# Folding adaLN's partial sums over partition halves with adding DMAs, and turning them later

## The chip, the cores and the metric

The kernel runs on one core of one Trainium2 chip. The metric is the device time of one execution in microseconds. The kernel before took 902.61 us, the median of three runs (901.67 to 902.88).

## The reference, cut to what matters

One layer over 256 tokens of width 2048 (D = 2048, E = 4096), in float32:

```python
h = rmsnorm(x, norm_g)
mod = silu(c) @ ada_w + ada_b            # (2048,) @ (2048, 6144)
shift, scale, gate = split(mod, 3)
h = h * (1 + scale) + shift
b_gate, c_gate, v, g = split(h @ w_in, 4)     # w_in: 2048 x 16384
y = b_gate * causal_conv3(c_gate * v) * silu(g)
x = x + gate * (y @ w_out)                    # w_out: 4096 x 2048
return rmsnorm(x, final_g)
```

The part that matters here is `silu(c) @ ada_w` for shift and scale: a product of one vector with a 2048 x 4096 matrix, whose result has to stand as one number for each channel, with the channels on the partitions, before the tokens of those channels can be multiplied with `w_in`.

## The kernel before, in words

TensorE works on float32 values split in two: a high part (a cast on ScalarE, `split_hi`) and a low part (a subtraction on VectorE, `split_lo`). Each product of a 128x128 weight block with a 128x256 token block is done three times: high weights with high tokens, high weights with low tokens, low weights with high tokens. `product` (line 526) issues one such matmul.

The 2048 input channels are 16 blocks of 128, called k = 0 to 15. adaLN's shift and scale are made in eight groups of two such blocks (`ADA`, k0 = 0, 2, ..., 14). The first group has code of its own; the other seven go through `ada_piece`, `ada_sums` and `ada_done`. For one group, `ada_w` comes in as eight pieces `at` (two 128-row slices each, lines 497 and 498, two DMAs for each piece on the SP queue). VectorE multiplies each slice by its 128 values of silu(c), one per partition, and adds it to `gv`, which is 128 partitions x 2 (shift, scale) x 256 channels (16 instructions for each group, lines 510 and 512). What is left is a sum over the 128 partitions. `ada_done` (line 514) does it by turning: four transposes on TensorE (line 519, one for each of shift and scale and for each of two channel blocks) put `gv` into the PSUM tile `tp_g` with channels on partitions, and VectorE sums the 128 columns of each (`reduce_sum`, line 521). `modulate` then adds the biases (line 348) and makes the tokens: two activations on ScalarE for the high tokens (line 352), and two instructions for each block on VectorE for the low ones (lines 356 and 359).

The main products over the first 16 column tiles of each quarter of `w_in` run in 16 banks (4 chunks `ch` x 4 quarters `q`), each in several parts: `plan()` (line 51 on) decides by its own costs which bank is worked on with which range k0:k1, so that banks run on whatever tokens are ready. A part is one opening of a PSUM bank; a bank that was opened before is seeded from `acc` (line 566) or added to it (line 555). These are 3072 matmuls, in the order in which `part` issues them, numbered 0 to 3071 below. Weights come in blocks of up to four k (48 matmuls), and `raw`, high and low parts have three buffers each.

By the plan, the tokens of group 8 (k = 8, 9) are first used by matmul 1128, those of group 10 by 1440, of group 12 by 1728 and of group 14 by 2016.

The order of the instructions on the queues around this is written out as strings of letters (lines 635 to 646). For VectorE: `s` is one addition to `gv`, `l` a low split, `r` the reduction of line 521, `m` the biases, `t` one of the four low-token instructions. For ScalarE: `h` is a high cast, `k` a copy of a bank to `acc`, `e` a seed, `t` a high-token activation. For SP: `w` is a load of weights and `a` one of adaLN's. Where the strings end or a kind is not in them, Tile's scheduler decides by its own timeline. That also holds for the place of the transposes among the matmuls, and for the last group's `r`, `m` and tokens.

GpSimd does nothing in this stretch. Later it folds the sums of the gate, which are needed on all partitions: seven rounds for each of four column groups, each round two DMAs on its own queue (lines 687 and 688, together all 256 KB of a tile moved to other partitions) and one addition (line 689).

Of the kernel before, what the change touches and what calls it, by code (L numbers as in the profile page):

```python
# [11 lines left out]
ALU = mybir.AluOpType  # L12

P = 128
# [103 lines left out]
def short_conv_layer(ctx: ExitStack, tc: tile.TileContext, x, c, norm_g, ada_w, ada_b, w_in, conv_w, w_out, final_g, out):  # L118
    nc = tc.nc
# [43 lines left out]
    after = mybir.DependencyInfo(mybir.DependencyClass.NoSync, mybir.DependencyReason.DATA)  # L163
# [26 lines left out]
    @contextmanager  # L190
    def of_kind(letter):

        traced = nc.cur_bb.bb.instructions
        n = len(traced)
        yield
        for ins in list(traced[n:]):
            lined_up.setdefault((ins.engine, letter), []).append(ins)

    def interleave(engine, letters):


        left = {k: iter(v) for (e, k), v in lined_up.items() if e == engine}
        front = None
        for letter in letters:
            ins = next(left[letter])
            if front is not None:
                tc.add_manual_dep(ins, front.name, after, reason="in the order of the letters")
            front = ins
# [52 lines left out]
    ident = const.tile([P, P], F32, tag="ident", name="ident")  # L261
# [99 lines left out]
    def modulate(k0, nk, sums):  # L361

        with of_kind("m"):
            add_biases(k0, nk, sums)
        with of_kind("t"):
            for k in range(k0, k0 + nk):
                high_tokens(k)
                low_tokens(k)
# [55 lines left out]
    for k in range(KT):  # L424
        c_k = silu_c[:, k : k + 1]
        at, gv = first_ada[k], gv0
        if k in ON_PE:
# [7 lines left out]
            at, gv = at[:, :, P : NK0 * P], gv0[:, :, P : NK0 * P]  # L435
# [45 lines left out]
        nc.vector.tensor_tensor(out=dst[:, :, 1, :], in0=y, in1=dst[:, :, 0, :].bitcast(F32), op=ALU.subtract)  # L481


    acc = {}
    sums = {}

    def ada_piece(k0, nk, piece):
        w = nk * P
        kk = ASLOT // (2 * w)
        if piece == 0:  # L490
            sums[k0] = adap.tile([P, 2, 2 * P], F32, tag="gv", name="gv")
        gv = sums[k0][:, :, 0:w]
        j = piece * kk
        at = adap.tile([P, ASLOT], F32, tag="at", name="at", bufs=4)
        at4 = at.rearrange("p (k s f) -> p k s f", k=kk, s=2)
        with of_kind("a"):
            for s in range(2):
                nc.sync.dma_start(at4[:, :, s, :], adas[:, j : j + kk, s, k0 * P : k0 * P + w])
        with later(GIVE), of_kind("s"):
            ada_sums(j, kk, at4, gv)  # L500
        if j + kk == KT:
            with later(-LEAD):
                ada_done(k0, nk, gv)
# [10 lines left out]
    def ada_done(k0, nk, gv):  # L514

        tp = psum.tile([P, 4, P], F32, tag="sm", name="tp_g", bufs=2)
        gs = const.tile([P, 4], F32, tag="gs", name="gs", bufs=2)
        for o in range(2 * nk):
            nc.tensor.transpose(tp[:, o, :], gv[:, o // nk, (o % nk) * P : (o % nk + 1) * P], ident)  # L519
        with of_kind("r"):  # L520
            nc.vector.reduce_sum(gs[:, 0 : 2 * nk], tp[:, 0 : 2 * nk, :], axis=mybir.AxisListType.X)
        modulate(k0, nk, gs[:, 0 : 2 * nk])

    opener = [None]

    def product(dst, hi, lo, k, i, begins, left, ends):

        w, h = ((hi, hh_), (hi, hl_), (lo, hh_))[i]

        mm = last_mm[0] = nc.tensor.matmul(dst, w, h[k], start=begins and left, stop=ends, skip_group_check=True)  # L530
        if begins and left:
            opener[0] = mm
        elif begins:
            tc.add_manual_dep(mm.ins, opener[0].ins.name, after, reason="the bank's flags are cleared first")

    def chunk_products(bank, hi, lo, o0, k, k0, k1, seed=False, late=False, parts=(0, 1, 2)):


        begins = k == k0 and not seed
        terms = [(m, i) for i in (0, 2, 1) for m in range(CT)] if late else [(m, i) for m in range(CT) for i in parts]  # L540
        for m, i in terms:
            o = slice(o0 + m * P, o0 + (m + 1) * P)
            product(bank[:, m, :], hi[:, o], lo[:, o], k, i, begins and i == 0, m % 2 == 0, 2 in parts and k == k1 - 1 and (m, i) == terms[-1])
# [72 lines left out]
    for kind, *step in plan():  # L616
# [15 lines left out]
                mixed(ch)  # L632


    interleave(mybir.EngineType.SP, (
        "wwaawaawaawaawwwaaaawwaaaawwaawaawaaaawaawwaawwaaaaaawwaawaaaaaawaawaawaaaawaawaawaaaawaawaawaawaaaa"
        "aawwaaaawaaaawwaaaawaawaaaawwaaaawaawaaaawaawaawaaaawaawaawaa"
    ))
    interleave(nc.vector.engine, (
        "lslsslslsslssllsslssllsssslslsrmslsttttslscsssslllssllssssssvlrmssltttstslssssslsslsslssssrlsmlsttst"  # L640
        "tslslsssssslslssslsrsmststttlslsssslslsssslslsrsmsslsttstltssslssslsslsssslsrmslsttttslsssslsslssls"
    ))
    interleave(nc.scalar.engine, (
        "hhhkxxxxhkhkkhkhhkhkhhkkhkhkhttkkhkhehhkhhkekehehkttekhekehkehkehkehkehttkhehkehhkhetthkhekehhkehhke"
        "htthkehhkehhkehtthkehhkhehkhehtthkehhkehhkehhkeh"
    ))

    ys.extend(slot([P, 2, 2, T], f"y{j}", F32R) for j in range(len(ys), NCT // 2))
# [72 lines left out]
    for ct in range(NS, NCT, 2):  # L721
        for q in QUARTERS:
            bank = psum.tile([P, CT, T], F32, tag="mm", name="mm_b")[:, 0:2]
            col = q * E + ct * P
            for kp in range(0, KT, KP):
                raw = raw_tile("raw")
                nc.sync.dma_start(
                    raw.rearrange("p (k f) -> p k f", k=KP),
                    w_in[0, kp * P : (kp + KP) * P, col : col + 2 * P].rearrange("(k p) f -> p k f", p=P),
                )  # L730
                hi, lo = split(raw, SLOT)
                for m in range(2):
                    for i in range(KP):
                        k = kp + i
                        o = slice((i * 2 + m) * P, (i * 2 + m + 1) * P)
                        for j in range(3):
                            product(bank[:, m, :], hi[:, o], lo[:, o], k, j, k == 0 and j == 0, m == 0, k == KT - 1 and j == 2)
                gate_piece()
# [137 lines left out]
    def wide_bank(name):  # L876
        return psum.tile([P, 2, W], F32, tag="mm", name=name)
# [32 lines left out]
    halves = [wide_bank("mm_o") for _ in range(2)]  # L910
# [89 lines left out]
```

## Time and profile before

| what | us |
|---|---|
| median of three runs | 902.61 |
| the profiled execution's own time | 902.57 |
| its span | 900.8 |
| TensorE busy | 887.4 (99%) |
| VectorE busy | 677.7 (75%) |
| ScalarE busy | 484.2 (54%) |
| GpSimd busy | 83.5 (9%) |

The page's names: PE is TensorE's matmuls, PEld its weight loads, DVE is VectorE, ACT ScalarE, POOL GpSimd, SP the queue that issues most DMAs. "Tenths" are rows of 40 digits, one for each fortieth of the span (22.5 us). A row of the timeline begins with the start and the duration, both in us, then engine, line, operation, output, input, and how many instructions were merged; square brackets at its end hold the idle time before it and what ended that. A row of the chain of work that ended last begins with start and duration too. Times in the text are counted from the start of the span.

### The profile page before, as it was taken

The numbers are of one execution on the slowest core, as the hardware profiler recorded it, in microseconds if no ns is written. First come the engines' busy times: TensorE is split into PE (matmuls) and PEld (weight loads), VectorE is DVE, ScalarE is ACT, GpSimd is POOL, SyncE is SP. The second block draws the span as 40 slices with busy tenths as digits, with TensorE's granted clock in tenths as the row PEclk, the third lists the DMA queues.
The fourth block names the chain that finished last, engine by engine and source line by source line (L and its number), as shares of the span: only waits on it lengthen the run. The fifth ranks groups of instructions, "written<-read, shape, count | busy, mean of one in ns | idle before, by whom it ended". The sixth has DMA issues, their size and how long they took to land.

```text
span 900.8 us, 16415 instructions
## 1 busy us (share of the span) xinstructions
PE 887.4 (99%) x6997; PEld 851.0 (94%) x6997; DVE 677.7 (75%) x667; ACT 484.2 (54%) x430; POOL 83.5 (9%) x95
## 2 busy tenths in 40 slices
PE   7999999999999999999999999999999999999996
PEld 4999999999999999999999999999999988888885
DVE  5899989888888867765965677555555568879896
ACT  6767966665558766644433434444434445554543
POOL 0000000000000134024234203320000000000000
PEclk9999999999999999999999999999999999999999
DMA  9999999999998588688888788766656476674662
GB/s 306 369 369 368 367 331 351 350 369 347 351 330 285 165 277 247 187 260 239 285 245 244 244 283 260 237 216 199 200 188 188 141 287 222 194 277 125 202 234 94
DMA packets 159610, 235.01 MB, mean 261 GB/s; under 512 B 6900, under 2 KB 105284, under 8 KB 159152
## 3 DMA queue, kind: packets, MB, share of 16 engines
q1 hardware_dynamic: 156368, 226.52, 76.6%
q0 software_dynamic: 3040, 7.39, 2.9%
q8 instruction: 55, 0.90, 0.4%
q14 instruction: 19, 0.16, 0.0%
q10 hardware_dynamic: 128, 0.04, 0.0%
HBM read 224.49 MB, written 2.10 MB: 252 GB/s over the span
## 4 chain that ended last, share of the span: by engine, by line
PE 95%; DMA 3%; DVE 1%; ACT 1%; issue 0%; SPq 0%; ACTq 0%
PE mm_s L530 39%; PE mm_b L530 39%; PE mm_w L793 7%; PE mm_o L793 6%; PE mm L793 4%; DMA at<-in_ada_w_dram 2%; DMA raw_o<-in_sc_w_out_dram 1%; PE tp_g L519 0%; PE sum L418 0%; ACT hi L380 0%; SPq L240 0%; DVE lo L824 0%; ACT hi L821 0%; DVE sums_o L816 0%; ACT big L907 0%
## 5 line engine op out<-in xcount | busy, mean ns | idle before, releaser
L530 PE MATMUL mm_b<-hT,hi 128*128 128x256 f32 x2048 | 348.2, 276 | 0.0
L530 PE MATMUL mm_s<-hT,hi 128*128 128x256 f32 x2048 | 336.6, 277 | 0.0
L530 PEld LDWEIGHTS mm_b<-hT,hi 128*128 128x128 f32 x2048 | 308.2, 188 | 0.0
L530 PEld LDWEIGHTS mm_s<-hT,hi 128*128 128x128 f32 x2048 | 299.1, 188 | 0.2
L530 PE MATMUL mm_b<-hT,lo 128*128 128x256 f32 x1024 | 282.6, 276 | 0.0
L530 PE MATMUL mm_s<-hT,lo 128*128 128x256 f32 x1024 | 261.8, 277 | 0.0
L385 DVE TENSOR_TENSOR lo<-raw,hi 128x2048 fp32r<-128x2048 f32 (+1 forms) x66 | 153.3, 2324 | 101.3 <-ACT hi L380 100.8
L380 ACT CAST hi<-raw 128x2048 fp32r<-128x2048 f32 (+1 forms) x66 | 123.7, 1875 | 192.7 <-PE mm_b L530 144.0
L530 PEld LDWEIGHTS mm_b<-hT,lo 128*128 128x128 f32 x1024 | 192.2, 188 | 0.0
L530 PEld LDWEIGHTS mm_s<-hT,lo 128*128 128x128 f32 x1024 | 182.5, 188 | 0.0
L385 DVE TENSOR_TENSOR lo<-raw_s,hi 128x2048 fp32r<-128x2048 f32 (+1 forms) x80 | 150.4, 1887 | 35.5 <-ACT hi L380 34.9
L380 ACT CAST hi<-raw_s 128x2048 fp32r<-128x2048 f32 (+2 forms) x81 | 124.0, 1540 | 59.4 <-PE mm_s L530 51.4
L512 DVE SCALAR_TENSOR_TENSOR gv<-at,silu_c,gv 128x512 f32<-128x512 f32 x105 | 78.6, 749 | 4.8 <-DMA at<-in_ada_w_dram 3.1
L552 ACT COPY acc<-mm_s 128x1024 f32<-128x1024 f32 x54 | 54.7, 1014 | 38.8 <-PE mm_s L530 38.7
L385 DVE TENSOR_TENSOR lo<-raw_o,hi 128x2048 fp32r<-128x2048 f32 x22 | 50.4, 2291 | 22.8 <-ACT hi L380 22.8
L380 ACT CAST hi<-raw_o 128x2048 fp32r<-128x2048 f32 x22 | 42.0, 1908 | 45.9 <-DMA raw_o<-in_sc_w_out_dram 10.1
L793 PE MATMUL mm_w<-hi,y 128*128 128x512 f32 x184 | 58.8, 389 | 0.0
L793 PE MATMUL mm_o<-hi,y 128*128 128x512 f32 x176 | 55.4, 389 | 0.0
L689 POOL TENSOR_TENSOR gacc<-gacc,z 128x512 f32<-128x512 f32 x28 | 42.3, 1511 | 105.5 <-DMA z<-gacc 105.5
L683 DVE SCALAR_TENSOR_TENSOR gacc<-at_g,silu_c,gacc 128x512 f32<-128x512 f32 x60 | 46.9, 781 | 6.5 <-DMA at_g<-in_ada_w_dram 5.3
L687 POOL DMA_DIRECT2D z<-gacc x28 | 15.5, 555 | 364.9 <-DVE acc L610 300.6
L793 PEld LDWEIGHTS mm_w<-hi,y 128*128 128x128 f32 x184 | 34.5, 188 | 7.1
(156 smaller groups left out, 687.9 us busy)
## 6 DMA issues: line engine op xcount, KB each, us to landing
raw<-in_sc_w_in_dram SPq DMA_DIRECT2D x64, 1024.0 KB, 5.8
raw_s<-in_sc_w_in_dram SPq DMA_DIRECT2D x47, 1024.0 KB, 7.8
raw_o<-in_sc_w_out_dram SPq DMA_DIRECT2D x32, 1024.0 KB, 5.3
at<-in_ada_w_dram SPq DMA_DIRECT2D x126, 256.0 KB, 7.7
raw_s<-in_sc_w_in_dram SPq DMA_DIRECT2D x33, 512.0 KB, 6.9
at_g<-in_ada_w_dram SPq DMA_DIRECT2D x32, 512.0 KB, 7.8
x<-in_x_dram SPq DMA_DIRECT2D x4, 512.0 KB, 6.4
big<-in_x_dram SPq DMA_DIRECT2D x2, 1024.0 KB, 8.2
```

The lines of the kernel that those rows point to most:

```text
L380: nc.scalar.copy(hi[:, :n], raw[:, :n])
L385: last_low[0] = nc.vector.tensor_tensor(out=lo[:, :n], in0=raw[:, :n], in1=hi[:, :n].bitcast(F32), op=ALU.subtract)
L512: nc.vector.scalar_tensor_tensor(out=gv, in0=at4[:, i], scalar=c_k, in1=gv, op0=ALU.mult, op1=ALU.add)
L530: mm = last_mm[0] = nc.tensor.matmul(dst, w, h[k], start=begins and left, stop=ends, skip_group_check=True)
L552: nc.scalar.copy(acc[ch, q], bank)
L683: nc.vector.scalar_tensor_tensor(out=ga, in0=at3[:, i, :], scalar=s, in1=ga, op0=ALU.mult, op1=ALU.add)
L687: nc.gpsimd.dma_start(turned[0 : P - away], ga[away:P])
L689: nc.gpsimd.tensor_tensor(out=ga, in0=ga, in1=turned, op=ALU.add)
L793: nc.tensor.matmul(dst, y[a], b, start=opens and i == 0, stop=ends and i == 2, skip_group_check=True)
```

## The change

For the last four groups (k0 = 8, 10, 12, 14; `FOLD = 8`) the 128 partial sums are first folded to 64. One DMA on GpSimd's queue adds the upper 64 partitions of the shift's sums to the lower 64. A second one adds the lower 64 partitions of the scale's sums to the upper 64. Each moves 64 rows of 1 KB. GpSimd then copies the folded scale (64 partitions x 256) beside the folded shift, into the partitions that became free. One transpose now turns shift and scale of one channel block together: two transposes for a group, where there were four. The reduction reads 256 columns of PSUM where it read 512.

The transposes of these groups get a fixed place: after the matmuls numbered 1034, 1284, 1534 and 1834, and ahead of the next one. In the written orders of VectorE and ScalarE the letters `r`, `m` and `t` of groups 8, 10 and 12 move back, behind some `s`, `l`, `h`, `k` and `e`; the order on SP stays.

```diff
+    FOLD = 8
+    TURNS = (1034, 1284, 1534, 1834)
+    turns = []
...
-        for o in range(2 * nk):
-            nc.tensor.transpose(tp[:, o, :], gv[:, o // nk, (o % nk) * P : (o % nk + 1) * P], ident)
+        if k0 >= FOLD:
+            h = P // 2
+            nc.gpsimd.dma_start(gv[0:h, 0], gv[h:P, 0], accum_op=ALU.add)
+            nc.gpsimd.dma_start(gv[h:P, 1], gv[0:h, 1], accum_op=ALU.add)
+            nc.gpsimd.tensor_copy(gv[h:P, 0], gv[h:P, 1])
+            turns.append([nc.tensor.transpose(tp[:, k, :], gv[:, 0, k * P : (k + 1) * P], ident) for k in range(nk)])
+            halves = tp[:, 0:nk, :].rearrange("p k (s f) -> p s k f", s=2)
+        else:
+            for o in range(2 * nk):
+                nc.tensor.transpose(tp[:, o, :], gv[:, o // nk, (o % nk) * P : (o % nk + 1) * P], ident)
+            halves = tp[:, 0 : 2 * nk, :].rearrange("p (s k) f -> p s k f", s=2)
         with of_kind("r"):
-            nc.vector.reduce_sum(gs[:, 0 : 2 * nk], tp[:, 0 : 2 * nk, :], axis=mybir.AxisListType.X)
+            nc.vector.reduce_sum(
+                gs[:, 0 : 2 * nk].rearrange("p (s k) -> p s k", s=2), halves, axis=mybir.AxisListType.X
+            )
...
+        products.append(mm)
...
+    for turned_rows, n in zip(turns, TURNS):
+        tc.add_manual_dep(turned_rows[0].ins, products[n].ins.name, after, reason="the folded sums are there")
+        tc.add_manual_dep(products[n + 1].ins, turned_rows[-1].ins.name, after, reason="no later")
...
     interleave(nc.vector.engine, (
         "lslsslslsslssllsslssllsssslslsrmslsttttslscsssslllssllssssssvlrmssltttstslssssslsslsslssssrlsmlsttst"
-        "tslslsssssslslssslsrsmststttlslsssslslsssslslsrsmsslsttstltssslssslsslsssslsrmslsttttslsssslsslssls"
+        "tslslsssssslslssslsssslrslmtststtsslslsssslslsssslssrlmssslttstsstlsslsssslsslsslrmssssttlttsslssls"
     ))
     interleave(nc.scalar.engine, (
-        "hhhkxxxxhkhkkhkhhkhkhhkkhkhkhttkkhkhehhkhhkekehehkttekhekehkehkehkehkehttkhehkehhkhetthkhekehhkehhke"
-        "htthkehhkehhkehtthkehhkhehkhehtthkehhkehhkehhkeh"
+        "hhhkxxxxhkhkkhkhhkhkhhkkhkhkhttkkhkhehhkhhkekehehkttekhekehkehkehkehkehttkhehkehhkhehkhettkehhkehhke"
+        "hhkehtthkehhkehhkttehhkhehkhehhketthhkehhkehhkeh"
     ))
```

More of the change, by code (lines that the diff above doesn't have):

```diff
@@ L517, in ada_done @@
         gs = const.tile([P, 4], F32, tag="gs", name="gs", bufs=2)
-        for o in range(2 * nk):
-            nc.tensor.transpose(tp[:, o, :], gv[:, o // nk, (o % nk) * P : (o % nk + 1) * P], ident)
+        if k0 >= FOLD:
[9 more added lines that the diff above has]
+            halves = tp[:, 0 : 2 * nk, :].rearrange("p (s k) f -> p s k f", s=2)
         with of_kind("r"):
-            nc.vector.reduce_sum(gs[:, 0 : 2 * nk], tp[:, 0 : 2 * nk, :], axis=mybir.AxisListType.X)
+            nc.vector.reduce_sum(
+                gs[:, 0 : 2 * nk].rearrange("p (s k) -> p s k", s=2), halves, axis=mybir.AxisListType.X
+            )
         modulate(k0, nk, gs[:, 0 : 2 * nk])
     opener = [None]
+    products = []
     def product(dst, hi, lo, k, i, begins, left, ends):
```

## The prediction, made before the result was known

> **What bounds the kernel now.** I read the page first: busy time, then the span in 40 slices.
>
> ```profile
> span 900.8 us, 16415 instructions
> PE 887.4 (99%) x6997; PEld 851.0 (94%) x6997; DVE 677.7 (75%) x667; ACT 484.2 (54%) x430; POOL 83.5 (9%) x95
> POOL 0000000000000134024234203320000000000000
> DMA  9999999999998588688888788766656476674662
> ```
>
> TensorE is busy 887.4 of 900.8 us, so almost every instruction taken off it shortens the span, and every wait put in front of it lengthens it. GpSimd shows no work in slices 2 to 13 (22 to 293 us), which hold the groups touched here. The DMA engines are full in just those slices. Next the chain of work that ended last, in order of time, for the place of each transpose; "x" counts matmuls, and no other engine appears in this stretch.
>
> ```profile
> 24.70 31.63 PE mm_s L530 x274
> ...
> 56.76 12.02 PE mm_s L530 x102
> 68.87 17.46 PE mm_s L530 x152
> ...
> 86.77 27.37 PE mm_s L530 x241
> ...
> 114.57 25.32 PE mm_s L530 x223
> 139.90 0.44 PE tp_g L519 x4
> 140.33 26.35 PE mm_s L530 x232
> ...
> 167.36 29.73 PE mm_s L530 x262
> ...
> 197.89 32.13 PE mm_s L530 x283
> ...
> 230.82 146.81 PE mm_s L530 x1295
> 377.63 348.16 PE mm_b L530 x3072
> ```
>
> Adding the counts numbers the matmuls: 274 + 102 + 152 + 241 + 223 = 992 stand ahead of group 8's transposes at 139.90 us; 232 more, 1224, ahead of group 10's; after a few mixed with single matmuls, 1491 are done at 197.89 and 1777 at 230.82. One matmul is 348.16 / 3072 = 0.1133 us, four transposes are 0.44 us (0.11 each). The new places are after numbers 1034, 1284, 1534 and 1834, some 43 to 60 matmuls (5 to 7 us) later.
>
> **The change, part by part.**
>
> (1) Fewer transposes. Eight go, 8 x 0.11 = 0.88 us off TensorE. There is no stall here to remove: from 24.70 to 377.63 TensorE is the chain throughout. Less work on VectorE follows:
>
> ```profile
> L519 PE MATMUL tp_g<-ident,gv x28: 270/272/273, 56.2 to 230.6; 128*128 128x128 f32 x28
> L521 DVE TENSOR_REDUCE gs<-tp_g x7: 683/691/692, 56.8 to 232.6; 128x4 f32<-128x512 f32 x7
> ```
>
> Half the columns make the reduction about 0.35 instead of 0.69 us, four times; VectorE isn't the bound, so nothing for the sum. (The 272 ns of one transpose is pipelined; the chain's 0.11 is what it adds.)
>
> (2) The fold, which is new on the path to the transposes. First its deadline, for group 8, from VectorE's timeline and ScalarE's:
>
> ```profile
> 136.14 0.74 DVE L512 SCALAR_TENSOR_TENSOR gv<-at,silu_c,gv 128x512 f32<-128x512 f32 x1
> 136.99 0.49 DVE L510 TENSOR_SCALAR gv<-at,silu_c 128x512 f32<-128x512 f32 x1
> ...
> 146.41 2.29 DVE L385 TENSOR_TENSOR lo<-raw_s,hi 128x2048 fp32r<-128x2048 f32 x1
> ```
> ```profile
> 143.48 1.09 ACT L352 ACTIVATE hT<-xs,mod 128x256 fp32r<-128x256 f32 x2 [3.44 <-DVE mod L348]
> 144.48 1.90 ACT L380 CAST hi<-raw_s 128x2048 fp32r<-128x2048 f32 x1
> ```
>
> The row at 136.99 opens group 10's sums, so group 8's last addition is the one at 136.14 and ends at 136.88. TensorE comes to its transposes after 43 matmuls more than before: 139.90 + 43 x 0.1133 = 144.8 (144.7 by the matmuls' own starts). So the fold has 7.8 us. Its pieces by their nearest rows, GpSimd's later folds of the gate:
>
> ```profile
> L689 POOL TENSOR_TENSOR gacc<-gacc,z x28: 1286/1295/3657, 313.7 to 591.3; 128x512 f32<-128x512 f32 x28
>   DMA z<-gacc: 105.5, 28
> ```
> ```profile
> L687 POOL DMA_DIRECT2D z<-gacc x28: 530/554/576, 310.7 to 586.5; - x28
> ```
> ```profile
> L688 POOL DMA_DIRECT2D z<-gacc x28: 502/510/524, 311.2 to 587.0; - x28
> DMA to landing us min/median/max: 2.3/4.1/8.7
> ```
> ```profile
> rows<-in_sc_conv_w_dram POOLq DMA_DIRECT2D x1, 48.0 KB, 5.5
> ```
> ```profile
> 137.00:141.00 4.00, 4.00 (x37) 4.00 (x36) 3.07 (x3) 3.04 (x3) 0.00 (x0) 1.00 1.06 376
> 141.00:145.00 4.00, 4.00 (x38) 4.00 (x37) 4.00 (x8) 1.52 (x3) 0.00 (x0) 1.00 1.08 364
> 545.00:562.00 17.00, 17.00 (x153) 17.00 (x152) 13.31 (x13) 6.79 (x5) 5.08 (x5) 1.00 0.92 276
> ```
>
> The first DMA is issued in 0.55 us; with some 0.2 us for the semaphore (an estimate; GpSimd's own turn-arounds are 0.3) the second starts at 137.65. From there 2.3, 4.1 or 8.7 us to landing: 139.9, 141.8 or 146.4. The DMA share (last column but one) says where in that range: 1.06 to 1.08 here, more than the 0.92 around the slowest gate folds (545 to 562 us). The one DMA that GpSimd issued in the crowded opening took 5.5 us for 48 KB. I take 5 us, 142.65. A gate pair moves 256 KB, this pair 128 KB, but an adding DMA also reads what it adds to, and no trace row shows one: it could be nothing dearer, or, if it serves its data twice, double. Then the copy: the addition of 512 columns and two inputs has 1.29 at least, the copy of 256 columns and one input should be half, 0.65 (0.3 to 1.3). It ends near 143.4, 1.3 us ahead of the deadline. I count this step at nothing; its cover is 42 matmuls, and beyond that each microsecond of delay is one of TensorE.
>
> A rule set against this. The Trainium skill, "DMA: Bandwidth & Descriptors", section "Anatomy of one DMA — SWDGE (gpsimd) path", prices such a DMA at 2.0 us plus bytes over 436e3, which for 64 KB is an estimate of 2.15 us. By it the fold would be in place near 140.5 and the sum would stay -0.88; by the slowest row above it would become a loss of about 1.4. The rows disagree with the rule, as their median is twice that.
>
> The other groups have more time. The last additions of groups 10, 12 and 14:
>
> ```profile
> 159.92 1.54 DVE L512 SCALAR_TENSOR_TENSOR gv<-at,silu_c,gv 128x512 f32<-128x512 f32 x2
> ...
> 189.67 0.74 DVE L512 SCALAR_TENSOR_TENSOR gv<-at,silu_c,gv 128x512 f32<-128x512 f32 x1
> ...
> 221.74 0.75 DVE L512 SCALAR_TENSOR_TENSOR gv<-at,silu_c,gv 128x512 f32<-128x512 f32 x1
> ```
>
> They end at 161.46, 190.41 and 222.49. The transposes come at 167.36 + 59 x 0.1133 = 174.0, 197.89 + 44 x 0.1133 = 202.9 and 230.82 + 58 x 0.1133 = 237.4, each less what the earlier groups have saved (up to 1 us): 11.5 to 14 us, against a fold of 0.75 + 8.7 + 0.65 = 10.1 at the slowest row. In group 12 the moved letters make VectorE up to 1.5 us later, which leaves 10. Nothing. On SP nothing is moved; the adding DMAs put some 0.5 MB into a stretch that moves 0.35 MB in each microsecond, 1.5 us over 100, behind loads that mostly wait for a free buffer. Nothing.
>
> (3) The later tokens. Group 8's are first used by matmul 1128, (1128 - 1035) x 0.1133 = 10.5 us after its new transposes. Behind these come the reduction, the biases, two activations and four vector instructions, queued behind at most one low split and one cast: about 5 us. The others have 17 us or more. Nothing.
>
> (4) The new order on VectorE. In group 8 it helps: the split at 146.41 stood behind the reduction and the tokens (and its cast at 144.48 behind ScalarE's wait of 3.44); now both pass them. The cast still needs the buffer that matmul 1007 frees, 140.33 + 16 x 0.1133 + 0.3 = 142.4, so the split can start at about 142.4 + 1.9 = 144.3, some 2 us earlier. That buffer is wanted by matmul 1080 at 140.33 + 88 x 0.1133 = 150.3, so VectorE was 1.6 us ahead and will be 3.6. In group 10 it hurts: the four token instructions (0.41 each) move to between two splits:
>
> ```profile
> 179.30 2.29 DVE L385 TENSOR_TENSOR lo<-raw_s,hi 128x2048 fp32r<-128x2048 f32 x1 [0.21 <-ACT hi L380]
> ...
> 183.75 2.28 DVE L385 TENSOR_TENSOR lo<-raw_s,hi 128x2048 fp32r<-128x2048 f32 x1
> ```
>
> The second ends at 186.03, is wanted by matmul 1416 at 167.36 + 190 x 0.1133 = 188.9, and becomes 1.65 us later: about 0.8 us stay. Nothing, but with little over.
>
> The sum: -0.88 + 0. Against the profiled execution's 902.57 (span 900.8 and 1.8 around it) that is 901.7; the profile lies 0.04 under the median of the three runs, so it holds for the median too.
>
> **The rivals.**
>
> (B) Group 8's fold is a little late. For: full DMA engines, an unknown price of adding. Against: 1.3 us of room. In its place a second mechanism makes the delay coarse: VectorE's next low split follows at about 144.3, by (4). In the gate's folds, GpSimd's addition took longest where such a split ran beside it:
>
> ```profile
> 548.35 3.66 POOL L689 TENSOR_TENSOR gacc<-gacc,z 128x512 f32<-128x512 f32 x1 [3.32 <-DMA z<-gacc]
> ```
> ```profile
> 548.56 2.28 DVE L385 TENSOR_TENSOR lo<-raw,hi 128x2048 fp32r<-128x2048 f32 x1
> ```
>
> It ended at 552.01, 1.17 after that split's end at 550.84, as if it had begun only then. So a copy that misses 144.3 ends near 144.3 + 2.3 + 0.5 = 147.1, a stall of 2.4: 901.7 + 2.4 = 904.1. The Trainium skill says the same in "SBUF — State Buffer", section "SBUF: two separate sides": VectorE with two SBUF inputs and a reading GpSimd instruction lock each other out for a whole instruction. By that rule this rival costs 2.4; without it, about 1 us less.
>
> (C) Slower: adding DMAs cost twice the plain ones. Place: TensorE ahead of group 8's transposes. With 2 x 5 us to landing the fold is there at 137.65 + 10 + 0.65 = 148.3 at the earliest, a stall of 3.6 and up to 2 more for a split in the way; groups 10 to 14 (0.75 + 10 + 0.65 = 11.4) just pass. 901.7 + 3.6 to 5.6 = 905.3 to 907.3. It decides from a landing of 9.2 us on, where the stall of 2.7 eats the gain and reaches 904.4. For: slices of full DMA. Against: only the data part, not the whole latency, should double.
>
> (D) Group 10's low split comes late, by letters. It decides from a delay of 0.8 us; price up to 1 us: 902.7.
>
> **How the numbers follow.** Forecast 0.50, B 0.25 (one in five of it over 904.4), C 0.15, D 0.06, and 0.04 for a gain that I see no place for. About 0.2% (1.8 us) is what a measurement of this kernel can tell from no change: under 900.8 is faster, over 904.4 slower. Forecast, D and most of B lie within, 0.76; C and the rest of B give 0.20; 0.04 faster. The range: below, the gain with the scatter of the three runs (0.6), 901.0; above, B's end, 904.6, which leaves C out.
>
> **What would show it.** Right: `tp_g` with 20 transposes instead of 28; four rows of GpSimd's copy, group 8's ending ahead of about 144.7; in the chain, TensorE unbroken from 24.70 to about 376.8; reductions of 0.35. B or C: TensorE with an idle time before `tp_g`, ended by GpSimd's copy, near 144.7, and landings of the adding DMAs over 6 us. D: an idle time near 188.5, ended by a low split. What would make it wrong outright is an adding DMA that is slower than any plain one here, in all four groups.

## The result, and the profile after

The changed kernel takes 907.18 us, the median of seven runs (906.1 to 912.0), against 902.36 before (901.67 to 902.98). The ratio is 1.0062, with a 95% interval of 1.0043 to 1.0081 (a ratio here compares single executions and isn't the quotient of the medians, which is 1.0053): 0.6% slower, where 901.7 was forecast, with a range of 901.0 to 904.6. The profiled execution took 906.1 us, 3.5 more than the profiled one before. It is the fastest of the seven, so 1.3 of the 4.8 us between the medians are not in its trace; the five slowest have a lower mean granted clock (0.994 to 0.996, where the two fastest have 0.997), which points to longer stretches at a low clock, but no trace of them was kept.

Two lines of the page of the changed kernel:

```profile
span 904.3 us, 16427 instructions
PE 888.7 (98%) x6989; PEld 851.7 (94%) x6989; DVE 674.4 (75%) x667; ACT 483.5 (53%) x430; POOL 101.3 (11%) x107
```

TensorE has eight instructions fewer, as it should, and is yet busy 1.3 us longer, beside 2.2 us more in which it isn't. The chain of work that ended last (start, duration, what) leaves TensorE around group 8, where it never did in the kernel before:

```profile
142.39 1.92 ACT hi L380
144.33 2.30 DVE lo L385
146.68 4.04 PE mm_s L545 x19
150.94 5.15 PE mm_s L545 x45
156.12 1.03 ACT acc L568
...
158.12 1.92 ACT hi L380
160.06 2.31 DVE lo L385
162.41 15.17 PE mm_s L545 x131
177.79 31.80 PE mm_s L545 x279
209.81 31.31 PE mm_s L545 x276
241.34 139.65 PE mm_s L545 x1232
380.99 348.36 PE mm_b L545 x3072
```

From 146.68 on, 19 matmuls take 4.04 us, 0.21 each where 0.113 is the rule. TensorE's timeline and its waits (us in total, times, longest) show what stands in front of them:

```profile
143.86 0.28 PE L545 MATMUL mm_s<-hT,lo 128*128 128x256 f32 x1
144.35 0.50 PE L545 MATMUL mm_s<-hT,hi 128*128 128x256 f32 x2 [0.22 <-ACT hi L380]
146.68 0.39 PE L545 MATMUL mm_s<-hT,lo 128*128 128x256 f32 x1 [1.82 <-DVE lo L385]
...
150.37 0.35 PE L545 MATMUL mm_s<-hT,lo 128*128 128x256 f32 x1
150.56 0.38 PE L526 MATMUL tp_g<-ident,gv 128*128 128x128 f32 x2
```
```profile
PE mm_s L545 <- DVE lo L385: 2.1, 2, 1.8
```

The wait isn't ahead of the transposes (`tp_g`, line 526 now), as the rivals B and C had it, but ahead of main products, and for a high cast and a low split. The order of TensorE's instructions in the two programs explains it. Matmul 1034 (the row at 143.86) is the last ahead of the transposes by the diff. In the built program Tile's scheduler put this there (each number in `mm_s_` is one bank; lines are in TensorE's order):

```
mm_s_1792<-hi_1795  x2
mm_s_1792<-lo_1796          matmul 1034
mm_s_1860<-hi_1863  x2      matmuls 1080, 1081: the next bank
mm_s_1860<-lo_1864
...                         18 more of the next bank, 1083 to 1100
tp_g<-gv            x2      group 8's transposes
mm_s_1792<-hi_1795          matmul 1035
```

So 21 matmuls of the next bank come between. (It also pulled 29 matmuls ahead of group 12's transposes and 5 ahead of group 14's; TensorE waits at neither in the trace.) In the kernel before they were 45 matmuls away, and VectorE had their weights 1.6 us ahead of them; here they are wanted at once:

```profile
142.39 1.91 ACT L380 CAST hi<-raw_s 128x2048 fp32r<-128x2048 f32 x1 [2.97 <-DMA raw_s<-in_sc_w_in_dram]
```
```profile
144.33 2.29 DVE L385 TENSOR_TENSOR lo<-raw_s,hi 128x2048 fp32r<-128x2048 f32 x1 [0.48 <-ACT hi L380]
```

The split ends at 146.62, and TensorE goes on at 146.68. The windows (length, busy time of PE, PEld, DVE, ACT and POOL, then the granted clock of TensorE, the DMA share, GB/s) give both halves of the loss:

```profile
143.80:146.70 2.90, 0.86 (x6) 0.46 (x5) 2.34 (x2) 2.90 (x4) 2.16 (x1) 1.00 1.07 372
146.70:150.50 3.80, 3.80 (x19) 3.80 (x20) 0.00 (x0) 0.37 (x1) 0.18 (x1) 0.55 1.08 364
161.80:163.00 1.20, 0.88 (x8) 0.68 (x7) 1.20 (x3) 1.07 (x2) 0.00 (x0) 1.00 0.07 19
```

TensorE stands still for 2.90 - 0.86 = 2.0 us. With the slow restarts, 2.6 us go there: from 143.86 to 146.91 four matmuls start, which take 4 x 0.1133 = 0.45 in a stream, 3.05 - 0.45. Then the granted clock is 0.55 in the mean of 3.8 us: 19 matmuls where 3.8 / 0.1133 = 33.5 fit, 14.5 x 0.1133 = 1.65 us. (It is 0.50 for 3.41 of them, see the last section.) Another 0.6 us go near 162, restart included. By the chain a low split is late there, because its cast stood behind the copy (`acc`, 156.12) of a bank that TensorE, itself late, had only then finished. That makes 4.9, less 0.9 for the eight transposes: 4.0. The measured difference of the two profiled executions is 3.5; 0.6 us of this gap lie ahead of group 8, as the chain goes on behind group 6's transposes at 113.94 here and at 114.57 in the kernel before.

The fold itself, GpSimd's timeline for group 8 and the copy for group 10, and the landings of all four second DMAs:

```profile
136.86 0.90 POOL L523 DMA_DIRECT2D gv<-gv  x1 [127.02 <-DVE gv L515]
137.45 1.17 POOL L524 DMA_DIRECT2D gv<-gv  x1
144.54 2.34 POOL L525 COPY gv<-gv 64x256 f32<-64x256 f32 x1 [5.93 <-DMA gv<-gv]
...
174.87 0.40 POOL L525 COPY gv<-gv 64x256 f32<-64x256 f32 x1 [5.50 <-DMA gv<-gv]
```
```profile
DMA to landing us min/median/max: 6.1/6.7/7.2
```

Group 8's sums are folded at 146.88, 2.9 us behind the 144.0 at which TensorE had done matmul 1034. So there are two candidates for the loss, one hidden behind the other: the order (theory O: the 21 matmuls that were pulled ahead and their weights) and the fold (theory F: it would have held TensorE up at the same place for as long).

### The profile page after: what moved, and what is told of

Its sections match the earlier page's. It is cut to its first block, busy times and chain, and to the rows that moved or that the text cites. A ratio compares the mean times of both kernels' runs of the same rounds, so it can differ in the third digit from the quotient of the medians.

```text
span 904.3 us, 16427 instructions
## 1 busy us (share of the span) xinstructions
PE 888.7 (98%) x6989; PEld 851.7 (94%) x6989; DVE 674.4 (75%) x667; ACT 483.5 (53%) x430; POOL 101.3 (11%) x107
## 4 chain that ended last, share of the span: by engine, by line
PE 92%; DMA 4%; DVE 2%; ACT 1%; issue 1%; SPq 0%; ACTq 0%
PE mm_b L545 39%; PE mm_s L545 36%; PE mm_w L812 7%; PE mm_o L812 6%; PE mm L812 4%; DMA at<-in_ada_w_dram 2%; DMA raw_s<-in_sc_w_in_dram 1%; DVE lo L385 1%; ACT hi L380 1%; DMA raw_o<-in_sc_w_out_dram 1%; DVE gv L515 0%; PE sum L418 0%; SPq L240 0%; DVE lo L843 0%; ACT hi L840 0%
## 5 line engine op out<-in xcount | busy, mean ns | idle before, releaser
L708 POOL TENSOR_TENSOR gacc<-gacc,z 128x512 f32<-128x512 f32 x28 | 49.8, 1777 | 105.9 <-DMA z<-gacc 105.9
L582 ACT COPY mm_s<-acc 128x1024 f32<-128x1024 f32 x38 | 38.6, 1016 | 2.6 <-DVE acc L571 1.8
```

The source lines that it names most:

```text
L582: nc.scalar.copy(bank, acc[ch, q])
L708: nc.gpsimd.tensor_tensor(out=ga, in0=ga, in1=turned, op=ALU.add)
```

## The experiments

Each time stands beside runs of the kernel before on the same chip; the ratio is to those.

**The order kept, the fold as it is.**

```diff
+    for n in range(1000, 1900):
+        tc.add_manual_dep(products[n + 1].ins, products[n].ins.name, after, reason="as written")
     for turned_rows, n in zip(turns, TURNS):
```

> The changed kernel, with matmuls 1000 to 1900 held in the order in which the program issues them. Theory O (order): the loss comes from the 21 matmuls of the next bank that Tile's scheduler put ahead of group 8's transposes, and that wait for weights cast and split only at 146.6 us; with the order kept the gain is there, about 901.5. Theory F (fold): the fold is there only at 146.9 us, when TensorE comes to its transposes at 144.0, so it waits 3.0 us there, and then runs some 19 matmuls at half its clock (1.9 us): 902.4 - 0.9 + 4.9, about 906.4, as slow as the changed kernel.

Measured: 902.25 us beside 902.0, ratio 0.9998 (0.9989 to 1.0007). The loss is gone, as theory O says, but the gain isn't there, which it doesn't say. The waits, then GpSimd's and VectorE's timelines:

```profile
PE tp_g L526 <- POOL gv L525: 0.7, 1, 0.7
```
```profile
137.59 1.16 POOL L524 DMA_DIRECT2D gv<-gv  x1
144.57 0.39 POOL L525 COPY gv<-gv 64x256 f32<-64x256 f32 x1 [5.82 <-DMA gv<-gv]
```
```profile
145.03 2.29 DVE L385 TENSOR_TENSOR lo<-raw_s,hi 128x2048 fp32r<-128x2048 f32 x1 [1.04 <-ACT hi L380]
```

Now the fold is late at its transposes: the copy ends at 144.96, and with the restart about 1.0 us goes, which eats the 0.9. It isn't the 4.9 that theory F had forecast, for two reasons: this copy began before the next low split and took 0.39 us, and the short wait left the clock alone.

**The pulled order, no fold.** Four transposes for each group from sums that stand early, TensorE's order around group 8 as in the changed kernel.

```diff
-    FOLD = 8
+    FOLD = 16
...
+    pulled = [*range(1000, 1035), *range(1080, 1101), *range(1035, 1080), *range(1101, 1900)]
+    for a, b in zip(pulled, pulled[1:]):
+        tc.add_manual_dep(products[b].ins, products[a].ins.name, after, reason="the next bank's come first")
+    for turned_rows, (a, b) in zip(turns, ((1100, 1035), (1284, 1285), (1534, 1535), (1834, 1835))):
```

> No fold: four transposes for every group, whose sums stand at 136.3 us in group 8, but TensorE's order around group 8 as in the changed kernel (21 matmuls of the next bank, then the transposes, then the rest of the bank), everything else in the program's order, and the new written orders. Theory O: the same loss as in the changed kernel, about 2.5 us of waiting for the next bank's weights and 1.9 at half clock, 906 to 907. Theory F: no fold, no loss, about 902.4.

Measured: 906.66 us beside 902.0, ratio 1.0047 (1.0032 to 1.0062). Theory O's number, without any DMA or copy of a fold. Its windows and its wait are like those of the changed kernel:

```profile
144.70:146.80 2.10, 0.31 (x2) 0.10 (x1) 2.08 (x1) 2.06 (x3) 0.00 (x0) 1.00 1.06 379
146.80:150.30 3.50, 3.46 (x16) 3.47 (x17) 0.00 (x0) 0.56 (x1) 0.00 (x0) 0.52 1.09 361
```
```profile
PE mm_s L549 <- DVE lo L385: 2.1, 2, 1.8
```

Together with the kept order, this settles the loss: the pulled order alone makes it, and keeping the order removes it. As nothing is saved in this run, its 4.7 us stand against 4.8 + 0.9 = 5.7 in the changed kernel; the intervals of the two overlap, and whether 1 us of the loss has another source stays open.

**The late places and the moved letters, no fold.** `FOLD = 16`, the four transposes of groups 8 to 14 at the places of the diff.

```diff
-    FOLD = 8
+    FOLD = 16
...
+            if k0 >= 8:
+                turns.append(made)
```

> No fold, four transposes for every group, but at the changed kernel's places (after 1034, 1284, 1534, 1834), with its written orders. Both theories: 902.4, no change. A loss here would say that the later places or the moved letters cost by themselves.

Measured: 901.92 us beside 902.0, ratio 0.9998 (0.9989 to 1.0007), as expected by both. It says one thing more. Here the scheduler left the matmuls in the program's order around all four places. The same places with the fold pulled the next bank ahead.

**The fold without fixed places.**

```diff
-    TURNS = (1034, 1284, 1534, 1834)
+    TURNS = ()
```

> The changed kernel without the four fixed places: Tile's scheduler puts the folded transposes after matmuls 1092, 1276, 1565 and 1840, and around group 8 it leaves the matmuls in the program's order. If pulling the next bank's matmuls ahead is the cause, that loss of some 4 us is gone; but group 8's transposes come at 150.6 us, and its tokens, some 6 us behind, are wanted by matmul 1128 near 154.8: a wait of about 2 us. 902.0 - 0.9 + 2, about 903.1. If it is as slow as the changed kernel (907), the pulled matmuls are not the cause.

Measured: 905.33 us beside 902.2, ratio 1.0028 (1.0018 to 1.0038). Nothing is pulled ahead around group 8 now, so it takes the fold and the fixed place together to pull. My reading, argued and not shown, is that matmul 1035 was bound behind the transposes, these behind a fold that in the scheduler's timeline wasn't done, and it filled the gap with what was ready there. What is lost here is the wait for the later tokens, and for a low split queued behind them:

```profile
PE mm_s L545 <- DVE lo L385: 1.8, 1, 1.8
...
PE mm_s L545 <- DVE hT L359: 0.4, 1, 0.4
```

The 2 us were expected; the median is 2.2 us over my 903.1. The profiled execution took 903.72, the fastest of eight, so the rest isn't in its trace and stays open.

**The order kept, group 8 turned later.** As the first experiment, with

```diff
-    TURNS = (1034, 1284, 1534, 1834)
+    TURNS = (1074, 1284, 1534, 1834)
```

> As e1_kept, with group 8's transposes after matmul 1074 instead of 1034: TensorE gets there near 148.6 us, 1.7 behind the end of the copy. Both theories: no wait ahead of the transposes, eight transposes fewer, 901.5, a ratio of 0.999. If it is slower than before, there is a third cause, such as group 8's tokens, first used by matmul 1128 near 155 us, or the moved letters.

Measured: 902.76 us beside 902.0, ratio 1.0008 (0.9999 to 1.0016). A miss for both: no wait at group 8's transposes, but two others. TensorE's and GpSimd's timelines:

```profile
158.33 0.39 PE L545 MATMUL mm_s<-hT,lo 128*128 128x256 f32 x1 [0.67 <-DVE lo L385]
...
203.61 0.44 PE L526 MATMUL tp_g<-ident,gv 128*128 128x128 f32 x2 [1.56 <-POOL gv L525]
```
```profile
201.00 2.56 POOL L525 COPY gv<-gv 64x256 f32<-64x256 f32 x1 [5.36 <-DMA gv<-gv]
```

Group 8's tokens come so late that a low split behind them is late; and group 12's fold, issued 1.6 us later than in the first experiment (193.99 against 192.40) and caught by a split for its copy (2.56 us), misses matmul 1534. Of the places tried for group 8, 1034 is too early for its fold and 1074 too late for its tokens. A place between them was not run: by the waits of 0.7 and 1.2 us for the fold that this section shows at 1034, 6 to 11 matmuls later would do for the fold (an estimate), and the tokens would still come some 30 matmuls earlier than with 1074.

**The order kept around group 8 only.** `range(1000, 1110)` in place of `range(1000, 1900)`.

> The changed kernel with only matmuls 1000 to 1110 held in the program's order, so that nothing is pulled ahead of group 8's transposes, while Tile's scheduler still pulls matmuls of the next bank ahead of group 12's. If group 8 is the place of the whole loss, this is as fast as e1_kept, 902.3; if the pulls around group 12 cost too, it lies between that and 907.

Measured: 902.30 us beside 901.66, ratio 1.0008 (0.9997 to 1.0019). Within the interval the loss is all at group 8; the 16 matmuls that the scheduler still pulls ahead of group 12's transposes cost nothing that can be told. The wait for the fold, again at group 8:

```profile
PE tp_g L526 <- POOL gv L525: 1.2, 1, 1.2
```

**Copying DMAs in place of adding ones.** The changed kernel without `accum_op`.

```diff
-            nc.gpsimd.dma_start(gv[0:h, 0], gv[h:P, 0], accum_op=ALU.add)
-            nc.gpsimd.dma_start(gv[h:P, 1], gv[0:h, 1], accum_op=ALU.add)
+            nc.gpsimd.dma_start(gv[0:h, 0], gv[h:P, 0])
+            nc.gpsimd.dma_start(gv[h:P, 1], gv[0:h, 1])
```

> The changed kernel with the two DMAs of each fold copying instead of adding; half of the partial sums of groups 8 to 14 are left out of the result by it. It prices the adding. If adding is what makes the fold slow, landings fall from some 6.5 us to the gate folds' 4 and the issues from 0.8 and 1.1 us to 0.5; if the full DMA engines are, they stay near 6.5 us. The time itself stays near 907, since the order stays.

One run took 907.67 us. The issues of group 8's pair and the landings of the second DMAs:

```profile
137.36 0.56 POOL L523 DMA_DIRECT2D gv<-gv  x1 [126.39 <-DVE gv L513]
137.91 0.52 POOL L524 DMA_DIRECT2D gv<-gv  x1
```
```profile
DMA to landing us min/median/max: 6.2/6.5/7.1
```

Adding costs GpSimd 0.3 to 0.6 us more to issue, and nothing that can be told in the landing (6.1 to 7.2 with it, 6.2 to 7.1 without). So it isn't the adding that makes the fold slow. What is left is the full DMA engines, which is argued, as no run here empties them; the gate's folds in the kernel before agree with it: the second DMA issued at 311.2 us took 2.3 us to land, at a DMA share of 0.51, and the one at 552.8 took 8.7, at 0.98. This run has the same wait of 1.8 us as the changed kernel, but the clock stays up behind it:

```profile
145.60:147.70 2.10, 0.30 (x2) 0.09 (x1) 2.07 (x1) 2.10 (x3) 0.00 (x0) 1.00 1.04 377
147.70:151.50 3.80, 3.78 (x33) 3.78 (x34) 1.08 (x3) 0.41 (x1) 0.00 (x0) 1.00 1.08 359
```

It is no faster for that, because its other waits are longer: main products wait 4.4 us for splits and casts in all, against 2.3 in the changed kernel. Why they are longer in this one execution stays open.

**A version that keeps the gain.** The order kept, the fold for groups 10, 12 and 14 only, group 12 a little later:

```diff
-    FOLD = 8
-    TURNS = (1034, 1284, 1534, 1834)
+    FOLD = 10
+    TURNS = (1284, 1560, 1834)
```

> The order of matmuls 1000 to 1900 held as the program issues them; the fold for groups 10, 12 and 14 only, group 12's transposes after matmul 1560 instead of 1534; group 8 with four transposes from sums that are not folded. The theory that is left: folds are slow (some 6.5 us to landing, and a copy of 0.4 to 2.6 us), and each kept order loses what the fold is late. Here no place is ahead of its fold (171.0, 201.5 and 232.7 us in e1_kept), so six transposes are saved and nothing is lost: 902.0 - 0.66, about 901.4, ratio 0.9993. If it is not under before, the saved transposes are lost elsewhere.

Measured: 901.36 us beside 902.2, ratio 0.9989 (0.9980 to 0.9998): 0.1% under the kernel before, by an interval that barely leaves out no change, and about what the six transposes are worth (6 x 0.11 = 0.66). Its page and its transposes:

```profile
PE 886.9 (99%) x6991; PEld 850.2 (94%) x6991; DVE 674.5 (75%) x667; ACT 484.2 (54%) x430; POOL 95.8 (11%) x104
```
```profile
L526 PE MATMUL tp_g<-ident,gv x6: 272/272/272, 173.2 to 236.2; 128*128 128x128 f32 x6
```

TensorE is busy 0.5 us less than in the kernel before, and no wait ahead of a transpose or of a main product of this stretch is left in the trace.

## Why the prediction was wrong

(1) Eight transposes fewer, worth 0.88 us: right as far as the runs show it. Six of them should give 0.66 and gave 0.84 us in the last experiment (901.36 against 902.2), the same within its interval.

(2) The fold, "TensorE comes to its transposes after 43 matmuls more than before": this is the step that failed. It was counted at nothing and cost 4.8 + 0.9 = 5.7 us by the medians. The step took the matmuls around the place for granted. The diff binds matmul 1034 ahead of the transposes and 1035 behind them, and says nothing of 1080 to 1100, which belong to another bank and may go anywhere. The scheduler moved 21 of them in between, 45 matmuls too early for their weights; the run with that order and no fold is as slow, within the intervals (906.66). The section on the kernel before says that the scheduler decides wherever nothing is written. I had read the letters of VectorE and ScalarE one by one and asked of TensorE only where the transposes stand.

The sizes in this step were off too, and harmless in the changed kernel: the 5 us from the second DMA to the copy were 7.1 (144.54 - 137.45), and the copy of 0.65 us took 0.40 alone and 2.34 beside a split. With the order kept, this lateness is what eats the gain (0.7 and 1.2 us of waiting in two runs). The Trainium skill's fit for such DMAs ("DMA: Bandwidth & Descriptors", "Anatomy of one DMA — SWDGE (gpsimd) path"), an estimate of 2.15 us for 64 KB, is a third of what these landings took.

(3) "About 5 us" from group 8's transposes to its tokens: from 150.56 to 156.80 in the changed kernel, 6.2. "Nothing" for the cost held at 1034, not at 1074 or 1092.

(4) The new letters cost nothing by themselves (901.92 with them and no fold). Rival D's place near matmul 1416 lost no more than 0.1 us.

Rival B was seen as a mechanism: the copy that began at 144.54 ended at 146.88, 0.26 us behind the split that ended at 146.62. In the changed kernel nothing waited for it. Rival C had the size, 905.3 to 907.3, by a cause that the copying DMAs rule out. No rival named an order that changes on TensorE, or a clock that falls behind a wait.

## What to carry to other kernels

An order written out for some engines leaves the rest to the scheduler. A dependency that binds one instruction of a sequence behind something slow can make it run the next sequence first, so the neighbours have to be bound too, and the engine's order in the built program is to be read before a place is trusted. Where an engine is the bound, price the work around a new wait, not the wait alone: here the 21 matmuls moved by the fold's fixed place cost five times what the fold saved.

## What the runs showed of the hardware that I had not expected

A wait of TensorE can cost about twice its length. Behind one of 1.82 us the granted clock was 0.50 for 3.41 us in the changed kernel, and as long in the run without the fold. Behind a wait of 1.82 us in the run with copying DMAs, and in the one without fixed places, it stayed 1.00, so it isn't the length of the wait alone that decides.

The traces show what does. In the changed kernel the next change of the clock after 150.50 is its fall at the very end, at 901.44: 750.94 us later, 220 steps of 3.413. Counted back in such steps from the fall at the end (901.31, 903.91 and 896.95 us in the other three), the steps around the waits are these: two each of the changed kernel, of the run without the fold, of the one with copying DMAs and of the one without fixed places (columns as above):

```profile
143.68:147.09 3.41, 1.37 (x10) 0.97 (x9) 2.46 (x2) 3.39 (x4) 2.34 (x1) 1.00 1.07 374
147.09:150.50 3.41, 3.41 (x18) 3.41 (x18) 0.00 (x0) 0.00 (x0) 0.00 (x0) 0.50 1.08 361
143.55:146.96 3.41, 1.59 (x12) 1.24 (x12) 3.02 (x2) 3.37 (x4) 0.00 (x0) 1.00 1.07 373
146.96:150.37 3.41, 3.41 (x17) 3.41 (x18) 0.00 (x0) 0.41 (x1) 0.00 (x0) 0.50 1.09 360
142.74:146.15 3.41, 2.41 (x19) 2.00 (x18) 2.32 (x4) 2.71 (x3) 0.40 (x1) 1.00 1.07 353
146.15:149.56 3.41, 1.84 (x16) 1.84 (x17) 1.52 (x1) 1.96 (x3) 0.00 (x0) 1.00 1.06 372
156.26:159.67 3.41, 2.38 (x20) 2.14 (x18) 3.36 (x4) 3.41 (x3) 0.00 (x0) 1.00 1.01 344
159.67:163.08 3.41, 2.61 (x22) 2.61 (x23) 3.37 (x5) 3.13 (x3) 0.00 (x0) 1.00 0.86 240
```

In the first two kernels the wait lies in one step, which is idle for 2.04 and 1.82 of its 3.41 us, and the next step runs at half clock. In the other two kernels a border cuts the wait, no step is idle for more than 1.57, and the clock stays. The ends of the traces agree: a step idle for 1.81 us is not followed by half clock (897.09 with copying DMAs), one of 2.21 is (893.54 without fixed places). So in these executions a step that was idle for about half of its length or more halved the clock of the next one, and where the borders fell decided what a wait cost.

The Trainium skill, "TensorE: Matmul & The Clock Gate", "What's actually happening", has the clock halve after an idle window of about 3.4 us, in windows that run on regardless of the kernel. The two levels, the slow stretch of 3.41 us and the steps agree with that; that 1.82 us of idling within a step are enough does not agree with a window that has to be idle throughout.

An adding DMA between partition halves landed as fast as a copying one (6.7 and 6.5 us in the median), while the DMA engines were full.
